# Token tiles of the output projection transposed by DMA in two planes of halves, in place of TensorE

## The chip, the core and the metric

The kernel runs on one core of a Trainium2 chip. The metric is the device time in microseconds, as the median of several runs. The core has a matrix engine (TensorE; PE in the profile, its weight loads PEld), a vector engine (VectorE, DVE), a scalar engine (ScalarE, ACT), GpSimd (POOL) and a queue for transfers (SyncE, SP). Each engine works its own instructions in the order in which they stand, and waits for the others by semaphores. Sixteen DMA engines serve the transfers that SP and ACT issue.

## What is computed

One decoder layer on 256 tokens of width 2048: a SwiGLU half-step, a token mixer of two recurrences (GLA and HGRN2), and a second SwiGLU half-step, each between two RMS norms. The change lies at the end of the mixer:

```python
merged = (sigmoid(z_gla + b[0]) * (o_gla @ w_branch_gla)
          + sigmoid(z_hgrn + b[1]) * (o_hgrn @ w_branch_hgrn))
return merged @ w_out          # (256, 2048) @ (2048, 2048)
```

All matrices and activations are float32.

## The kernel before

**Products.** The 256 tokens are two tiles t = 0, 1 of 128 rows. A product in float32 is made of three matmuls of 128x128 against 128x512 (`mm3`, L158 to L160): every operand is split into a high part in the matrix engine's own format (`hi`, a copy on ACT, L152) and the rest (`lo`, a subtraction on DVE, L154). The weights arrive from DRAM as `raw` (512 KB for 128x1024, issued by SP at L134) and are split into `whi` and `wlo`. Each of the three has a ring of five buffers (`RING`). A weight buffer of 128x1024 is called a chunk here; it feeds twelve matmuls.

**The stage.** `gemm_block` computes the second branch's product `o_hgrn @ w_branch_hgrn` in four blocks n = 0 to 3 of 512 columns: four chunks, 48 matmuls into two banks of PSUM (`mm`, t = 0, 1). After each block, `merge(t, n, b)` runs for both t: at L1257 it multiplies the bank `b` by the gate `s` (tile `sz`) on DVE, at L1258 it adds the other branch's tile `m` (which lies in the home of `h`), both 128x512. So `s` holds merged tokens by columns.

**Transposing.** The output projection `out_proj` needs those tiles with the columns of the model on the partitions, as `xhi` and `xlo` of `mT`. `to_T` makes four transposes on PE against an identity matrix (L398) into a bank of PSUM, and splits that bank: `xhi` on ACT, `xlo` on DVE. A pair of tiles (t = 0, 1) thus costs eight transposes. Then `merge` reloads `h` from its copy in DRAM (L1261, issued by ACT, 256 KB), since `m` lay in its place.

**The projection.** `out_proj` runs 24 chunks (inner tile `kt` 0 to 11 for two halves `hf` of the columns), loaded, split and used in turn, and a tail of eight chunks for `kt` 12 to 15. It accumulates into the eight banks `acc`. `lhs` for tile `kt` pumps the side work until the columns of `kt` are transposed; block n gives `kt` = 4n to 4n + 3.

**What sets the order.** Each engine's queue is set by a scheduler at build time; the kernel's loops give it the program, and the generators in `Side` are stepped between the chunks: `pump` moves each of the light ones by one `yield`, `flush` runs them all to their end. Before the change, `out_proj` calls `side.flush()` once, after its second chunk.

**The pattern that exists already.** In both FFNs `finish` turns the SwiGLU tiles into `hT` by DMA: ACT copies the float32 tile, seen as 16-bit halves, into two planes (`halves`: first all low halves, then all high ones, L708); a transposing DMA of 16-bit elements, issued by ACT, writes `turned` (L712); six steps later ACT copies the planes back, interleaved (`hT`, L717). There are 44 such tiles.

Of the kernel before, what the change touches and what calls it, by code (L numbers as in the profile page):

```python
# [7 lines left out]
F32 = mybir.dt.float32  # L8
# [3 lines left out]
U16 = mybir.dt.uint16  # L12
AF = mybir.ActivationFunctionType
# [3 lines left out]
P = 128  # L17
# [6 lines left out]
CB = 512  # L24
# [63 lines left out]
def kernel(ctx: ExitStack, tc: tile.TileContext, a: dict, out: bass.AP):  # L88
    nc = tc.nc
    side = Side()  # L90
# [7 lines left out]
    work = ctx.enter_context(tc.tile_pool(name="work", bufs=2))  # L98
# [5 lines left out]
    def nm(s):  # L104
        uid[0] += 1
        return f"{s}_{uid[0]}"

    def ps_tile(s="ps"):
        return psum.tile([P, CB], F32, tag="ps", name=nm(s))

    h = [[hpool.tile([P, CB], F32, name=f"h{t}_{n}") for n in range(4)] for t in range(NT)]
# [25 lines left out]
    def wchunk(src: bass.AP, w: int, alloc=ring_alloc, raw=None):  # L137


        raw, apart = raw or wload(src, w)  # L140
        parts = alloc(w)
        if len(parts) == 1:
            hi, lo = parts[0]
            for i in range(2) if apart else [slice(0, 2)]:
                split_into(hi[:, i, :], lo[:, i, :], raw[:, i, :])
            return [(hi[:, i, :], lo[:, i, :]) for i in range(2)]
        for i, (hi, lo) in enumerate(parts):
            split_into(hi, lo, raw[:, i, :])
        return parts

    def split_into(hi, lo, src):
        last[0] = nc.scalar.activation(hi, src, AF.Copy)  # L152
        with tc.issue_after(first_ops.pop().ins) if first_ops else nullcontext():
            nc.vector.tensor_tensor(lo, src, hi.bitcast(F32), op=ALU.subtract)  # L154

    def mm3(ps, x, w, start, stop):
        (xhi, xlo), (whi, wlo) = x, w
        nc.tensor.matmul(ps, lhsT=xhi, rhs=whi, start=start, stop=False)  # L158
        nc.tensor.matmul(ps, lhsT=xlo, rhs=whi, start=False, stop=False)  # L159
        nc.tensor.matmul(ps, lhsT=xhi, rhs=wlo, start=False, stop=stop)  # L160
# [219 lines left out]
    def row_tile(s, dt=F32):  # L380
        return rows.tile([P, 3, CB], dt, tag="row", name=nm(s))

    def load_bcast(t, name, n, after):

        with tc.issue_after(after.ins):
            nc.scalar.dma_start(t, a[name][:, n * CB:(n + 1) * CB].broadcast_to([P, CB]))
# [9 lines left out]
    def transpose4(dst_ps, src, n=4):  # L396
        for i in range(n):
            end = nc.tensor.transpose(dst_ps[:, i * P:(i + 1) * P], src[:, i * P:(i + 1) * P],  # L398
                                      ident)
        return end  # L400

    def tiles4(x):
        return x.rearrange("p (k c) -> p k c", c=P)

    def new_xT():
        x = [None] * NT, [None] * NT, [0] * NT
        for t in range(NT):
            alloc_xT(x, t)
        return x

    def alloc_xT(x, t):
        for part, s in zip(x, ("xhi", "xlo")):
            part[t] = tpool.tile([P, KT, P], F32R, tag=f"{s}{t}", name=nm(f"{s}{t}"))
# [8 lines left out]
    def to_T(x, t, n, src, col=None):  # L422


        ps = ps_tile()
        transpose4(ps, src)
        sl = slice(4 * n, 4 * n + 4)
        v = tiles4(ps)
        if col is not None:
            v = tiles4(work.tile([P, CB], F32, tag="tmp", name=nm("u"), bufs=3))  # L430
            nc.vector.tensor_tensor(v, tiles4(ps), col[:, sl].unsqueeze(2).broadcast_to([P, 4, P]),
                                    op=ALU.mult)
        split_into(x[0][t][:, sl, :], x[1][t][:, sl, :], v)
        x[2][t] = 4 * n + 4
# [100 lines left out]
    def out_proj(w_dram, nkt, lhs, post, scale, pre, homes, following):  # L535

        acc = [[None] * 4 for _ in range(NT)]  # L540
        wpost, free = [], []
        nxt, rs, ready = ([None] * NT, [None] * NT, [0] * NT), [None, None], []

        def load(kt, hf, alloc=ring_alloc):
            return wchunk(w_dram[kt * P:(kt + 1) * P, hf * 1024:(hf + 1) * 1024]
                          .rearrange("p (n c) -> p n c", n=2), CB, alloc)

        def mm(t, n, kt, parts):
            if acc[t][n] is None:
                acc[t][n] = ps_tile(f"acc{t}{n}")  # L550
            mm3(acc[t][n], lhs(t, kt), parts[n % 2], kt == 0, kt == nkt - 1)

        order = [(kt, hf) for hf in range(2) for kt in range(2)]
        order += [(kt, hf) for kt in range(2, nkt - TAIL) for hf in range(2)]
        for i, (kt, hf) in enumerate(order):
            parts = load(kt, hf)
            if 6 <= i < 10:

                if not free:
                    t3 = row_tile("row")  # L560
                    free += [t3[:, j, :] for j in range(3)]
                wpost.append(free.pop(0))
                load_bcast(wpost[-1], post, i - 6, last[0])
            for t in range(NT):
                for n in (2 * hf, 2 * hf + 1):
                    mm(t, n, kt, parts)
            if i == 1:
                side.flush()
        tail = [[(kt, load(kt, hf, homes[hf * TAIL + i]))
                 for i, kt in enumerate(range(nkt - TAIL, nkt))] for hf in range(2)]  # L570

        for t in range(NT):
            ss = small.tile([P, 4], F32, tag="ss", name=nm("ss"))
            for n in range(4):
                for i, (kt, parts) in enumerate(tail[n // 2]):
                    mm(t, n, kt, parts)
                    if i == TAIL // 2 - 1:
                        side.pump()
                square(acc[t][n], ss, n)

                nc.vector.tensor_tensor(acc[t][n], acc[t][n], wpost[n], op=ALU.mult)
                if following is not None and t == 0 and n < AHEAD:
                    ready.append(following(n))
                side.pump()
            side.spawn(settled(t, acc, ss, scale, pre, nxt, rs))
        return nxt, rs, ready
# [89 lines left out]
    def ffn(pre, x, rs, post, pre_next, begin=None, ready=(), then=None):  # L676
        with ExitStack() as fctx:
            fwork = fctx.enter_context(tc.tile_pool(name=nm("fwork"), bufs=2, reuse_waits="tile"))
# [19 lines left out]
            hT = []  # L698
# [3 lines left out]
            def finish(t, f0, w, u, s):  # L702
                n = w // P
                nc.vector.scalar_tensor_tensor(s[:, :w], u[:, :w], rs[t], s[:, :w],
                                               op0=ALU.mult, op1=ALU.mult)
                yield
                halves = fwork.tile([P, 2 * CB], U16, tag="halves", name=nm("halves"))
                nc.scalar.activation(halves[:, :2 * w].rearrange("p (h f) -> p h f", h=2),  # L708
                                     s.bitcast(U16)[:, :2 * w].rearrange("p (f h) -> p h f", h=2),
                                     AF.Copy)  # L710
                turned = work.tile([P, 8, P], U16, tag="tmp", name=nm("turned"), bufs=3)
                nc.scalar.dma_start_transpose(turned[:, :2 * n, :], halves[:, :2 * w])  # L712
                for _ in range(6):
                    yield
                dst = hT[f0 // CB].bitcast(U16)[:, :n, 2 * t * P:2 * (t + 1) * P]
                src = turned[:, :2 * n, :].rearrange("p (h j) k -> p h j k", h=2)
                nc.scalar.activation(dst.rearrange("p j (k h) -> p h j k", h=2), src, AF.Copy)  # L717

            for f0 in range(0, DFF, CB):
                w = min(CB, DFF - f0)  # L720
# [11 lines left out]
                s = []  # L732
# [60 lines left out]
    def mixer(x, rs, ready, following):  # L793
        xl = lhs_of(x)
        w_in = a["w_in"]
        with ExitStack() as mctx:
# [5 lines left out]
            def blk(s, dt=F32):  # L802
                return b2.tile([P, CB], dt, tag="b", name=nm(s), bufs=33)
# [307 lines left out]
            def cols(c0):  # L1111
                return first_of(w_in, c0)
# [64 lines left out]
            k, v, ready = two(O_GK, O_GV, (), cols(O_GV + CB), cols(O_GO))  # L1177
# [8 lines left out]
            go, f, ready = two(O_GO + CB, O_HF, ready, cols(O_HI), cols(O_HO), late=True)  # L1186
# [27 lines left out]
            q, f, ready = two(O_HQ + CB, O_HF + CB, ready, cols(O_HI + CB), cols(O_HO + CB), late=True)  # L1214
# [38 lines left out]
            mT = new_xT()  # L1253

            def merge(t, n, b):
                s, m = szs[n][t], ms[n][t]
                nc.vector.tensor_tensor(s, b, s, op=ALU.mult)  # L1257
                nc.vector.tensor_tensor(s, m, s, op=ALU.add)  # L1258
                yield
                to_T(mT, t, n, s)  # L1260
                nc.scalar.dma_start(m, away[t][n])  # L1261

            side.until(lambda: not side.heavy)
            for n in range(4):
# [105 lines left out]
```

## Time and profile before

| what | us |
|---|---|
| median of 3 runs | 2069.73 (2069.12 to 2075.82) |
| the profiled execution | 2072.41 |
| its span | 2070.3 |
| second branch product, blocks n = 0 to 3, begin at | 1247.15, 1258.15, 1269.93, 1281.73 |
| output projection begins at | 1293.51 |
| the 32 transposes of `sz` lie between | 1260.9 and 1299.7 |

A row of the profile's timeline gives start and length in us from the span's start, engine, line, operation, output and input tile, count, and in brackets the idle time of the engine ahead of it with what ended it. Rows of groups give count, busy us, the mean ns of one, and the idle time with its releasers. PE's lengths overlap, since matmuls are pipelined: the starts tell its pace.

### The profile page before, as it was taken

How to read it: one execution, taken by the hardware profiler on the slowest of the kernel's cores; microseconds unless marked ns; L12 is line 12 of the kernel's file. 1: busy time of each engine (PE TensorE's matmuls, PEld its weight loads, DVE VectorE, ACT ScalarE, POOL GpSimd, SP SyncE). 2: the span in 40 equal slices, each digit the busy share in tenths (PEclk: the TensorE clock that was granted, in tenths of full speed). 3: DMA queues.
4: the chain of work that ended last, by engine and by line, in shares of the span. 5: the costliest groups of instructions: out<-in, count | busy, mean ns of one | idle time of the engine just before them, and what ended most of it. 6: DMA issues, size and time to landing. Idle time of an engine off the chain costs nothing. (4 is left out here: it accounts for less than half of the span.)

```text
span 2070.3 us, 28990 instructions
## 1 busy us (share of the span) xinstructions
PE 2054.9 (99%) x10337; PEld 1701.7 (82%) x10337; DVE 1849.8 (89%) x2187; ACT 1303.3 (63%) x1714; POOL 40.7 (2%) x87
## 2 busy tenths in 40 slices
PE   9999999999999999999999999999999999999998
PEld 7888888888888888878888888888888888888886
DVE  7899998998999879989999897577998999989996
ACT  6666666666666576576655554465666666666663
POOL 1000000000000100000000000010000000000000
PEclk9999999999999999999999999999999999999999
DMA  8776767767667467556565566756767767686663
GB/s 268 204 221 209 242 187 222 217 189 236 212 197 229 153 193 231 163 169 191 171 200 192 180 220 216 220 187 183 219 212 210 214 213 244 176 239 196 217 209 130
DMA packets 246105, 423.50 MB, mean 205 GB/s; under 512 B 63476, under 2 KB 71863, under 8 KB 245960
## 3 DMA queue, kind: packets, MB, share of 16 engines
q1 hardware_dynamic: 194896, 401.80, 61.6%
q10 hardware_dynamic: 51064, 19.84, 4.8%
q8 instruction: 81, 1.33, 0.3%
q14 instruction: 64, 0.52, 0.1%
HBM read 406.11 MB, written 4.19 MB: 198 GB/s over the span
## 5 line engine op out<-in xcount | busy, mean ns | idle before, releaser
L154 DVE TENSOR_TENSOR wlo<-raw,whi 128x1024 fp32r<-128x1024 f32 (+3 forms) x498 | 586.0, 1191 | 83.6 <-ACT whi L152 82.5
L152 ACT ACTIVATE whi<-raw 128x1024 fp32r<-128x1024 f32 (+3 forms) x498 | 507.1, 1031 | 228.9 <-PE c L159 66.2
L158 PE MATMUL c<-whi,xhi 128*128 128x512 f32 (+1 forms) x1270 | 494.0, 389 | 0.0
L160 PE MATMUL c<-wlo,xhi 128*128 128x512 f32 (+1 forms) x1270 | 490.7, 387 | 0.4 <-DVE wlo L154 0.4
L159 PE MATMUL c<-whi,xlo 128*128 128x512 f32 (+1 forms) x1270 | 490.4, 386 | 0.0
L244 DVE TENSOR_TENSOR wlo<-raw,whi 128x1024 fp32r<-128x1024 f32 (+1 forms) x252 | 295.9, 1204 | 35.9 <-ACT whi L283 23.1
L160 PEld LDWEIGHTS c<-wlo,xhi 128*128 128x128 f32 x1270 | 238.4, 188 | 48.0 <-DVE wlo L154 0.9
L158 PEld LDWEIGHTS c<-whi,xhi 128*128 128x128 f32 x1270 | 238.4, 188 | 46.6 <-ACT xhi L470 0.6
L159 PEld LDWEIGHTS c<-whi,xlo 128*128 128x128 f32 x1270 | 238.5, 188 | 45.6
L283 ACT ACTIVATE whi<-raw 128x1024 fp32r<-128x1024 f32 (+1 forms) x126 | 131.6, 1044 | 199.1 <-DVE raw L244 99.6
L244 DVE TENSOR_TENSOR wsuml<-wsum,wsumh 128x1536 fp32r<-128x1536 f32 (+1 forms) x126 | 217.9, 1729 | 8.1 <-ACT wsumh L285 8.1
L160 PE MATMUL c<-wlo,hkhi 128*128 128x512 f32 x558 | 217.2, 389 | 2.4 <-DVE wlo L154 2.0
L159 PE MATMUL c<-whi,hklo 128*128 128x512 f32 x558 | 216.9, 389 | 0.2 <-DVE hklo L154 0.2
L158 PE MATMUL c<-whi,hkhi 128*128 128x512 f32 x558 | 216.8, 389 | 0.0
L281 ACT ACTIVATE wsumh<-wsum 128x1024 fp32r<-128x1024 f32 (+1 forms) x126 | 131.1, 1040 | 88.3 <-DVE wsum L244 65.9
L279 ACT ACTIVATE whi<-raw 128x1024 fp32r<-128x1024 f32 (+1 forms) x126 | 130.9, 1039 | 60.0 <-PE c L159 44.9
L244 DVE TENSOR_TENSOR wsum<-raw,raw 128x1024 f32<-128x1024 f32 (+1 forms) x126 | 151.7, 1204 | 17.8 <-DMA raw<-in_ffn_w_down_dram 13.1
L160 PEld LDWEIGHTS c<-wlo,hkhi 128*128 128x128 f32 x558 | 104.7, 188 | 25.4 <-DVE wlo L154 2.4
L159 PEld LDWEIGHTS c<-whi,hklo 128*128 128x128 f32 x558 | 104.7, 188 | 22.2 <-DVE hklo L154 0.6
L158 PEld LDWEIGHTS c<-whi,hkhi 128*128 128x128 f32 x558 | 104.7, 188 | 21.4
L244 DVE TENSOR_TENSOR c<-c,psum 128x512 f32<-128x512 f32 (+1 forms) x135 | 86.4, 683 | 10.6 <-PE c L160 10.4
L244 DVE TENSOR_TENSOR wsum<-raw 128x512 f32<-128x512 f32 (+1 forms) x126 | 86.1, 683 | 3.6
(346 smaller groups left out, 3156.8 us busy)
## 6 DMA issues: line engine op xcount, KB each, us to landing
raw<-in_ffn_w_down_dram SPq DMA_DIRECT2D x124, 512.0 KB, 5.1
raw<-in_w_in_dram SPq DMA_DIRECT2D x104, 512.0 KB, 4.5
raw<-in_ffn_w_up_dram SPq DMA_DIRECT2D x97, 512.0 KB, 4.4
raw<-in_ffn_w_gate_dram SPq DMA_DIRECT2D x96, 512.0 KB, 4.7
raw<-in_ffn_w_gate_dram SPq DMA_DIRECT2D x128, 256.0 KB, 4.0
raw<-in_w_in_dram SPq DMA_DIRECT2D x128, 256.0 KB, 3.5
raw<-in_ffn_w_up_dram SPq DMA_DIRECT2D x126, 256.0 KB, 3.8
raw<-in_ffn_w_down_dram SPq DMA_DIRECT2D x96, 256.0 KB, 3.6
```

The source lines that it names most:

```text
L152: last[0] = nc.scalar.activation(hi, src, AF.Copy)
L154: nc.vector.tensor_tensor(lo, src, hi.bitcast(F32), op=ALU.subtract)
L158: nc.tensor.matmul(ps, lhsT=xhi, rhs=whi, start=start, stop=False)
L159: nc.tensor.matmul(ps, lhsT=xlo, rhs=whi, start=False, stop=False)
L160: nc.tensor.matmul(ps, lhsT=xhi, rhs=wlo, start=False, stop=stop)
L244: return nc.vector.tensor_tensor(o, x, y, op=op)
L279: nc.scalar.activation(ahi, ra, AF.Copy)
L281: nc.scalar.activation(hi[:, 0:2, :], wsum[:, 0:2, :], AF.Copy)
L283: nc.scalar.activation(bhi, rb, AF.Copy)
```

## The change

Two helpers are taken out of `finish`, and `merge` uses them in place of `to_T`. `turn` is the split into planes and the transposing DMA, `joined` the copy back. In `merge` the copy goes back into `s` itself, three steps later, and `s` is then split into `xhi` and `xlo`. The FFN's instructions stay as they were. In `out_proj` one `pump` after every chunk but the first takes the place of the flush after the second. The tile `halves` comes from the mixer's pool of 33 blocks, `turned` from the pool of three that the FFN uses too.

```diff
+    def turn(src, halves):
+        w = src.shape[-1]
+        halves = halves.bitcast(U16)[:, :2 * w]
+        nc.scalar.activation(halves.rearrange("p (h f) -> p h f", h=2),
+                             src.bitcast(U16).rearrange("p (f h) -> p h f", h=2), AF.Copy)
+        turned = work.tile([P, 8, P], U16, tag="tmp", name=nm("turned"), bufs=3)
+        turned = turned[:, :2 * w // P, :]
+        nc.scalar.dma_start_transpose(turned, halves)
+        return turned
+
+    def joined(dst, turned):
+        nc.scalar.activation(dst.bitcast(U16).rearrange("p j (k h) -> p h j k", h=2),
+                             turned.rearrange("p (h j) k -> p h j k", h=2), AF.Copy)
...
-            if i == 1:
-                side.flush()
+            if i:
+                side.pump()
...
                 nc.vector.tensor_tensor(s, m, s, op=ALU.add)
                 yield
-                to_T(mT, t, n, s)
+                turned = turn(s, blk("halves"))
                 nc.scalar.dma_start(m, away[t][n])
+                yield
+                yield
+                yield
+                joined(tiles4(s), turned)
+                sl = slice(4 * n, 4 * n + 4)
+                split_into(mT[0][t][:, sl, :], mT[1][t][:, sl, :], tiles4(s))
+                mT[2][t] = 4 * n + 4
```

In the changed file the split into planes stands at L409, the transposing DMA at L413, the copy back at L418, the reload of `h` at L1270.

The next rows are ACT's queue before, from the last weight split ahead of the first pair (n = 0) on. `h_0_81` and `h_0_85` are the reloads, `ps` the banks with the transposed tiles.

```order
L152 ACTIVATE whi_11991<-raw_11989 128x1024
L1261 DMA h_0_81<-away_0_89 128x512
L1261 DMA h_0_85<-away_0_93 128x512
L152 ACTIVATE whi_12025<-raw_12023 128x1024
L152 ACTIVATE xhi_2392_11799<-ps_11913 128x512
L152 ACTIVATE xhi_2394_11801<-ps_11921 128x512
L152 ACTIVATE whi_12043<-raw_12041 128x1024
```

And now, at the same place, from the same split on; the `whi` that follow are called A (`whi_12019`) and B.

```order
L152 ACTIVATE whi_11991<-raw_11989 128x1024
L409 ACTIVATE halves_11913<-sz_11039 128x1024
L1270 DMA h_0_81<-away_0_89 128x512
L413 DMA_TRANSPOSE turned_11915<-halves_11913 128x8x128
L409 ACTIVATE halves_11918<-sz_11400 128x1024
L1270 DMA h_0_85<-away_0_93 128x512
L413 DMA_TRANSPOSE turned_11920<-halves_11918 128x8x128
L418 ACTIVATE sz_11039<-turned_11915 128x2x512
L152 ACTIVATE whi_12019<-raw_12017 128x1024
L152 ACTIVATE xhi_2392_11799<-sz_11039 128x512
L418 ACTIVATE sz_11400<-turned_11920 128x2x512
L152 ACTIVATE whi_12037<-raw_12035 128x1024
```

The copy back (L418) waits for a transposing DMA issued just ahead of it, and the weight splits A and B stand behind such copies. Behind B stand the second `xhi`, the splits C and D, and the second pair, built the same way with E and F.

ACT's queue at the third pair (n = 2), now: `turned_12103` and `turned_12108` are its two tiles, G is `whi_12149`, H to J are the three at the end.

```order
L413 DMA_TRANSPOSE turned_12103<-halves_12101 128x8x128
L409 ACTIVATE halves_12106<-sz_11789 128x1024
L1270 DMA h_2_87<-away_2_95 128x512
L413 DMA_TRANSPOSE turned_12108<-halves_12106 128x8x128
L152 ACTIVATE whi_12149<-raw_12147 128x1024
L418 ACTIVATE sz_11410<-turned_12103 128x2x512
L418 ACTIVATE sz_11789<-turned_12108 128x2x512
L152 ACTIVATE xhi_2392_11799<-sz_11410 128x512
L152 ACTIVATE xhi_2394_11801<-sz_11789 128x512
L152 ACTIVATE whi_12177<-raw_12175 128x1024
L152 ACTIVATE whi_12199<-raw_12197 128x1024
L152 ACTIVATE whi_12227<-raw_12225 128x1024
```

One weight split stands between issue and copies; before, this place had the two reloads, one `whi`, the two `xhi` and three `whi`, as at the first pair. At the fourth pair two weight splits (K, L) stand between the issues and the copies, and M is the first behind its `xhi`.

On PE the eight groups of transposes are gone. Those of the fourth pair stood in the output projection, before:

```order
L158 MATMUL acc_2467_12193<-whi_12199,xhi_2394_11801 128x512
L159 MATMUL acc_2467_12193<-whi_12199,xlo_2395_11802 128x512
L160 MATMUL acc_2467_12193<-wlo_12200,xhi_2394_11801 128x512
L398 MATMUL ps_12215<-ident,sz_11412 128x128 x4
L398 MATMUL ps_12223<-ident,sz_11794 128x128 x4
L158 MATMUL acc_2476_12237<-whi_12233,xhi_2392_11799 128x512
```

Now the projection begins so, with the products of `whi` of several accumulators ahead of those of `wlo`:

```order
L158 MATMUL acc_2473_12193<-whi_12177,xhi_2394_11801 128x512
L159 MATMUL acc_2473_12193<-whi_12177,xlo_2395_11802 128x512
L158 MATMUL acc_2484_12231<-whi_12227,xhi_2392_11799 128x512
L159 MATMUL acc_2484_12231<-whi_12227,xlo_2393_11800 128x512
L158 MATMUL acc_2485_12235<-whi_12227,xhi_2392_11799 128x512
L159 MATMUL acc_2485_12235<-whi_12227,xlo_2393_11800 128x512
L160 MATMUL acc_2470_12181<-wlo_12178,xhi_2392_11799 128x512
```

No row between them is a transpose, and four matmuls of the chunk J (`whi_12227`) are drawn ahead of the `wlo` products of H.

More of the change, by code (lines that the diff above doesn't have):

```diff
@@ L706, in finish @@
                 yield
[L707 to L712, printed above, removed]
+                turned = turn(s[:, :w], fwork.tile([P, CB], F32, tag="halves", name=nm("halves")))
                 for _ in range(6):
                     yield
-                dst = hT[f0 // CB].bitcast(U16)[:, :n, 2 * t * P:2 * (t + 1) * P]
-                src = turned[:, :2 * n, :].rearrange("p (h j) k -> p h j k", h=2)
-                nc.scalar.activation(dst.rearrange("p j (k h) -> p h j k", h=2), src, AF.Copy)
+                joined(hT[f0 // CB][:, :n, t * P:(t + 1) * P], turned)
             for f0 in range(0, DFF, CB):
```

## The prediction

> **What bounds the kernel now.** The first two parts of the page come first: is one engine full, and at what clock?
>
> ```profile
> span 2070.3 us, 28990 instructions
> ...
> PE 2054.9 (99%) x10337; PEld 1701.7 (82%) x10337; DVE 1849.8 (89%) x2187; ACT 1303.3 (63%) x1714; POOL 40.7 (2%) x87
> ...
> PEclk9999999999999999999999999999999999999999
> ```
>
> TensorE (PE) is busy in 99% of the span at full clock. So a PE instruction that goes is time won, and every microsecond that PE waits is time lost: no later slack takes it back. The change touches one stage, the four blocks of the second branch product and the start of the output projection. The view by windows gives that stage, with one row for each block and two for pieces of the projection (columns: length, then busy time and count of PE, PEld, DVE, ACT and POOL, clock, DMA share, GB/s).
>
> ```profile
> 1258.15:1269.93 11.78, 11.78 (x58) 9.84 (x56) 8.49 (x11) 5.22 (x6) 0.00 (x0) 1.00 0.72 222
> 1269.93:1281.73 11.80, 11.80 (x57) 9.84 (x56) 8.48 (x11) 5.22 (x6) 0.00 (x0) 1.00 0.75 225
> 1281.73:1293.51 11.78, 11.78 (x58) 9.84 (x56) 8.49 (x11) 5.22 (x6) 0.00 (x0) 1.00 0.73 223
> 1293.51:1316.14 22.63, 22.63 (x104) 18.58 (x103) 13.01 (x14) 9.46 (x10) 0.00 (x0) 1.00 0.79 249
> 1316.14:1337.90 21.76, 21.76 (x97) 18.02 (x96) 9.81 (x8) 8.49 (x8) 0.00 (x0) 1.00 0.63 196
> ```
>
> PE is busy from end to end in every row, and ACT less than half of each. The busy share of ACT hides a limit, though: ACT works its queue in order, and the next rows show how far ahead of PE it is.
>
> ```profile
> 1255.46 1.06 ACT L152 ACTIVATE whi<-raw 128x1024 fp32r<-128x1024 f32 x1 [1.66 <-PE mm L159]
> 1258.18 1.06 ACT L152 ACTIVATE whi<-raw 128x1024 fp32r<-128x1024 f32 x1 [1.66 <-PE mm L159]
> 1259.68 0.94 ACTq L1261 DMA_DIRECT2D h<-away  x2
> 1260.90 1.06 ACT L152 ACTIVATE whi<-raw 128x1024 fp32r<-128x1024 f32 x1 [1.66 <-PE mm L159]
> ```
>
> Each weight split `whi` waits for PE to free a place in the ring of five, so ACT runs at PE's pace, one `whi` every 2.72 us. The one at 1260.90 refills the place of the chunk that PE began at 1258.15. PE needs it five chunks later, at 1258.15 + 5 x 2.72 = **1271.75**: some 9.8 us after it is written. That is the cushion into which new ACT work falls.
>
> **What the change removes.** The transposes of the first pair stand so on PE:
>
> ```profile
> 1260.65 0.39 PE L160 MATMUL mm<-wlo,oT 128*128 128x512 f32 x1
> 1260.88 1.03 PE L398 MATMUL ps<-ident,sz 128*128 128x128 f32 x8
> 1261.67 0.48 PE L158 MATMUL mm<-whi,oT 128*128 128x512 f32 x1
> 1261.98 0.40 PE L159 MATMUL mm<-whi,oT 128*128 128x512 f32 x1
> 1262.22 0.39 PE L160 MATMUL mm<-wlo,oT 128*128 128x512 f32 x1
> ```
>
> Undisturbed matmuls start 0.227 us apart (48 of them: 10.88 us). A block with eight transposes takes 11.78 or 11.80, thus 0.90 more, and the projection's piece with eight 22.63 against 21.76, thus 0.87. Four groups: 0.90 + 0.92 + 0.90 + 0.87 = **3.6 us**, all on the path. The eight copies of `xhi` and eight `xlo` stay, only with another source.
>
> A rule of the Trainium skill (VectorE: DVE Perf Modes, "Rules for kernel authors") speaks against this change: it sends a 128x128 transpose to TensorE where PSUM may be the destination, and otherwise to the DMA. The same page's section "The three transpose paths" puts the former at 390 ns; 32 of them would be an estimated 12.5 us, and the sum below would come out 1.3 us faster than before. The windows say 0.11 us for each, and the measurement decides.
>
> **What it adds.** Per pair of tiles (t = 0, 1) ACT gets two splits into planes (`halves`), two transposing DMAs, and two copies back (`sz<-turned`, here J0 and J1). Both FFNs do the same to `hT`, so these rows have their durations, from the views by tile of `halves` and `turned`:
>
> ```profile
> L708 ACT ACTIVATE halves<-silu x44: 828/1042/1060, 55.3 to 1837.1; 128x1024 uint16<-128x1024 uint16 x40, 128x768 uint16<-128x768 uint16 x4
> L712 ACTq DMA_TRANSPOSE turned<-halves x44: 1227/1292/2006, 56.3 to 1838.5; - x44
> L717 ACT ACTIVATE hT<-turned x44: 1062/1361/1394, 61.7 to 1847.5; 128x1024 uint16<-128x1024 uint16 x40, 128x768 uint16<-128x768 uint16 x4
> DMA to landing us min/median/max: 2.8/5.1/8.9
> ```
>
> So 1.04 us for a split, 1.29 for an issue (which must wait for its split, and holds what stands behind it), 1.36 for a copy, and between issue and landing L = 2.8 to 8.9, median 5.1. Even without a wait this fills ACT: 2 x (1.04 + 1.29 + 1.36) for the pair, 4 x 0.96 for the `whi` and 2 x 0.53 for the `xhi` are 12.3 us a block against PE's 10.88. And on top ACT **waits** for each landing, with the next `whi` queued behind. In the FFN such a wait looks like this:
>
> ```profile
> 1562.57 1.39 ACT L717 ACTIVATE hT<-turned 128x1024 uint16<-128x1024 uint16 x1 [0.45 <-DMA turned<-halves]
> 1566.10 1.37 ACT L717 ACTIVATE hT<-turned 128x1024 uint16<-128x1024 uint16 x1 [2.14 <-DMA turned<-halves]
> 1567.33 1.03 ACT L152 ACTIVATE whi<-raw 128x1024 fp32r<-128x1024 f32 x1
> ```
>
> There three or four splits stand between issue and copy. Here, by the new order of ACT's queue, none does in the first two pairs, one in the third, two in the fourth.
>
> I follow that queue. An instruction behind another on ACT starts about 0.1 us before the first one's end (`whi` at 1250.02 for 1.06, the next at 1250.98), so the steps are 0.96 for `whi`, 1.26 for J, 0.53 for `xhi` (two in 1.06).
>
> ```profile
> 1250.02 1.06 ACT L152 ACTIVATE whi<-raw 128x1024 fp32r<-128x1024 f32 x1
> 1250.98 0.62 ACT L1027 ACTIVATE sz<-sz 128x512 f32<-128x512 f32 x1
> ...
> 1261.86 1.06 ACT L152 ACTIVATE xhi<-ps 128x512 fp32r<-128x512 f32 x2
> ```
>
> From a pair's start: split 1.04, issue to 2.33, second split to 3.37, second issue to 4.66.
> - Pair 0: J0 at 1.04 + L, `whi` A, `xhi`, J1 at 3.79 + L, `whi` B, `xhi`, `whi` C and D; the next pair begins at 8.46 + L.
> - Pair 1: the same with two `whi` (E, F): 6.54 + L.
> - Pair 2: `whi` G during the wait, J0, J1 at 3.37 + L (its own DMA left 2.33 later), two `xhi`, `whi` H, I, J: 8.57 + L.
> - Pair 3: `whi` K and L, J0, J1 at 3.37 + L, two `xhi`, and `whi` M is done at 6.75 + L.
>
> Pair 0 starts at 1259.68, where ACT now sends the reload of `h`, which waits for the same sum. M is done at 1259.68 + 30.3 + 4L. PE wants M twelve chunks after A, at 1271.75 + 12 x 2.72 = 1304.4. Behind M stands its `wlo` on DVE (1.22 us), which PE wants 0.45 after M: 0.77 more. Together **PE is late by 4L - 13.6 us**. With L = 5.1 that is 6.8: 1.7 for F, 1.2 for G, 3 for H, the rest for M. Each microsecond of landing counts four times, since four waits stand in a row on one queue. The next rows are the stage's groups on DVE, and from the list of DMA issues the reload of `h`.
>
> ```profile
> L154 DVE TENSOR_TENSOR wlo<-raw,whi 128x1024 fp32r<-128x1024 f32 x25 | 30.5, 1224 | 22.7 <-ACT whi L152 22.7
> L154 DVE TENSOR_TENSOR xlo<-ps,xhi 128x512 fp32r<-128x512 f32 x8 | 5.1, 683 | 0.0
> ...
> h<-away ACTq DMA_DIRECT2D x8, 256.0 KB, 3.5
> ```
>
> DVE's own queue adds nothing: the sum that pair 1 needs stands behind `xlo` of pair 0 and is done at about 7.9 + L, before 8.46 + L; the same margin holds later.
>
> **Which L.** The trace has no transpose of `sz`. From below, 2.8 us; from above, 8.9. I take 5.1 and add 1.1, because each transpose has a reload of `h` just ahead in ACT's DMA queue: 256 KB at the stage's 223 GB/s, an estimate. L = 6.2 makes PE late by 11.2, less 3.6 removed: **7.6 us slower**. Should the cushion not be there, each pair would cost PE the wait in full; it is in the formula as the 13.6.
>
> **Edits at nothing.** Stepwise pumping in place of the flush only moves the last pair's splits: its columns (inner tile 12 on) are read after 24 chunks of the projection, 65 us on. FFN lines only call the new helpers; same instructions. The eight transposes (2 MB) add about a tenth of what the stage's DMA moves, and its share is 0.72 to 0.79.
>
> **Rivals.**
> 1. *The transposes land fast and the cushion holds* (not slower). With L up to 3.4 the formula gives no lateness, only the removal is left: 3.6 us faster, 2066. For it: a plain DMA of the same 256 KB from the same queue lands in 3.5, and the fastest transposes in 2.8. Against it: the median of 5.1 under weight traffic of the same strength. The Trainium skill (Advanced Engine Details and Errata, "X-Bar Transpose (TRN2)") says that transposing DMAs are as fast as regular ones; that rule is this rival, and this trace, 5.1 against 3.5, speaks against it. The sides change at L = 4.3, where the lateness equals the 3.6 us removed.
> 2. *The transposes land late.* After a wait ACT frees several raw buffers at once, SP sends that many 512 KB weight loads, and they share the engines with the next transpose. At L = 8 PE is late by 18.4, and the kernel 14.8 us slower: 2084.5. For it: landings up to 8.9, where a pair is sent into running loads. Against it: here a pair's DMAs leave 2.3 us apart, not 1.3.
>
> That the change doesn't do what it says is no rival: all eight groups of transposes are gone from PE's queue.
>
> **How the numbers follow.** The profiled execution took 2072.41, its span 2070.3; the median of three runs is 2069.73, 2.7 lower. The forecast gives 2072.41 + 7.6 = 2080.0 for such an execution, and 2069.73 + 7.6 = 2077.3 on the median's scale, which I use. About 0.3%, 6.2 us, is what a measurement of this kernel can tell from no change; the forecast passes that at L = 5.84. Chances: forecast (L 4.3 to 7.4, nothing to 12.4 slower) 0.65, rival 1 0.18, rival 2 0.17. Slower by over 0.3%: all of rival 2 and 0.38 of the forecast, 0.55. Within 0.3%: 0.43. Faster by over 0.3% would need more than all that is removed: 0.02. The range 2066.5 to 2086 reaches from rival 1 to L = 8.4 and leaves out the ends of both.
>
> **What would show it.** Right: in the windows from 1269 to 1312 blocks longer than 10.88, the lateness beginning with the third block; ACT idle before `sz` on the copy's line, ended by the DMA `turned`; PE waiting for `whi` or `wlo` of L152 and L154; landings near 6. Wrong: all blocks at 10.88 and a span 3.6 shorter (rival 1), landings of 8 and weight loads in bursts (rival 2), or waits at another place, a PSUM bank or DVE. The forecast stands or falls with the eight landings.

## The result, and the profile after

| | median, us | runs |
|---|---|---|
| after | 2083.57 (2078.61 to 2086.99) | 6 |
| before, beside it | 2071.95 (2069.12 to 2076.2) | 6 |

The ratio is 1.0053, with a 95% interval of 1.0041 to 1.0066: the change costs 8.5 to 13.7 us. The forecast was 7.6 slower. The profiled execution of after took 2081.05 us. Its page begins with the span and then the busy time of the engines:

```profile
span 2078.9 us, 28953 instructions
...
PE 2055.8 (99%) x10305; PEld 1702.7 (82%) x10305; DVE 1849.4 (89%) x2187; ACT 1320.2 (64%) x1730; POOL 40.7 (2%) x87
```

The 32 transposes are gone (10337 matmuls before, 10305 now), and little else on the page tells that the kernel lost: PE still shows 99%, since some 10 us of waiting are half a per cent of the span. The view by windows tells it. Its rows for after are the four blocks, the wait ahead of the projection, and the projection up to its 192nd matmul in two pieces (columns as in the prediction).

```profile
1246.72:1257.73 11.01, 11.01 (x51) 9.10 (x50) 9.16 (x12) 6.97 (x10) 0.00 (x0) 1.00 0.60 185
1257.73:1268.61 10.88, 10.88 (x49) 9.01 (x48) 3.23 (x5) 3.18 (x3) 0.00 (x0) 1.00 0.94 152
1268.61:1283.96 15.35, 13.36 (x49) 9.91 (x48) 9.02 (x11) 9.53 (x11) 0.00 (x0) 0.89 0.65 156
1283.96:1301.07 17.11, 13.03 (x48) 9.67 (x47) 7.16 (x9) 9.96 (x11) 0.00 (x0) 0.90 0.87 206
1301.07:1304.15 3.08, 0.39 (x3) 0.01 (x1) 1.70 (x4) 3.08 (x5) 0.00 (x0) 1.00 0.37 118
1304.15:1328.76 24.61, 23.85 (x96) 18.95 (x96) 15.65 (x16) 15.28 (x16) 0.00 (x0) 0.93 0.86 270
1328.76:1350.52 21.76, 21.76 (x98) 18.02 (x96) 11.03 (x9) 9.55 (x9) 0.00 (x0) 1.00 0.75 247
```

The second block now takes 10.88, without transposes, and is still in step. The third takes 15.35, the fourth 17.11, and 3.08 more pass before the projection starts. From the first block's start to the end of the last row it is 103.80 us; before, from 1247.15 to 1337.90, it was 90.75. So the stage lost **13.05 us**, and PE, from which 3.6 us of transposes were taken, is 16.65 late. (The rest of the span, with the same 3229 matmuls, came out shorter in this execution: 728.38 against 732.40 before. In the traces of the other kernels of this study, which have the same instructions there, it is 729.3 to 733.1. So most of this difference is the spread between executions; that none of it comes from the change is not shown.)

The next rows are ACT's timeline in after, at the first pair:

```profile
1260.34 1.28 ACTq L413 DMA_TRANSPOSE turned<-halves  x1
...
1270.27 1.36 ACT L418 ACTIVATE sz<-turned 128x1024 uint16<-128x1024 uint16 x1 [7.54 <-DMA turned<-halves]
1271.50 1.03 ACT L152 ACTIVATE whi<-raw 128x1024 fp32r<-128x1024 f32 x1
```

The first transpose is issued at 1260.34, and ACT stands still for 7.54 us until it has landed. Only then comes the weight split, which PE wants by 1271.33 in this execution (its second block began at 1257.73; five chunks of 2.72 later). The list of waits says who waited in the stage from the first pair on, first for ACT (1259.2 to 1320.1), then for PE (1246.7 to 1328.8):

```profile
ACT sz L418 <- DMA turned<-halves: 17.4, 5, 7.5
ACT halves L409 <- DVE wlo L154: 4.1, 3, 1.4
ACT whi L152 <- issue: 2.8, 2, 1.5
ACT halves L409 <- DVE sz L1267: 1.8, 2, 1.3
```

```profile
PE acc L158 <- ACT whi L152: 3.2, 2, 2.7
PE mm L160 <- DVE wlo L154: 3.2, 3, 2.3
PE mm L158 <- ACT whi L152: 2.9, 2, 1.8
PE acc L160 <- DVE wlo L154: 0.3, 1, 0.3
```

ACT waits 17.4 us for landings and not once for PE; the three other rows are mostly the time in which it issues a DMA (mostly 1.25 to 1.43 us each, not counted as busy). Before, it waited mostly for PE, 16.6 us of it in this row of the same view (1259.2 to 1305):

```profile
ACT whi L152 <- PE mm L159: 16.6, 10, 1.7
```

So the roles are exchanged: in this stage ACT's queue sets the pace and PE follows. How long a transfer took stands in the list of DMA issues for 1258 to 1318 (count of issues, and the median from the start of the issue to the landing):

```profile
turned<-halves ACTq DMA_TRANSPOSE x8, 7.4
```

Eight transposes were issued, but the records have the landing of only five: 9.9, 8.4, 5.2, 5.6 and 7.4 us. A sixth can be read from the copy that waited for it: the transpose issued at 1278.58 was awaited until 1283.76, thus 5.2. The median of these six is 6.5, not 7.4. (Of the other two, the one issued at 1293.15 was shorter still: its copy began at 1297.80 without a wait.) So every landing given below comes with the number of landings that it rests on.

### The profile page after: what moved, and what is told of

Same layout as the page of the kernel before. It is cut to its first block, busy times and chain, and to the rows that moved or that the text cites. A ratio compares the mean times of both kernels' runs of the same rounds, so it can differ in the third digit from the quotient of the medians.

```text
span 2078.9 us, 28953 instructions
## 1 busy us (share of the span) xinstructions
PE 2055.8 (99%) x10305; PEld 1702.7 (82%) x10305; DVE 1849.4 (89%) x2187; ACT 1320.2 (64%) x1730; POOL 40.7 (2%) x87
## 5 line engine op out<-in xcount | busy, mean ns | idle before, releaser
L154 DVE TENSOR_TENSOR wlo<-raw,whi 128x1024 fp32r<-128x1024 f32 (+3 forms) x498 | 585.3, 1190 | 83.4 <-ACT whi L152 79.8
L152 ACT ACTIVATE whi<-raw 128x1024 fp32r<-128x1024 f32 (+3 forms) x498 | 506.2, 1030 | 205.2 <-PE c L159 71.7
L244 DVE TENSOR_TENSOR wsum<-raw,raw 128x1024 f32<-128x1024 f32 (+1 forms) x126 | 151.6, 1203 | 17.9 <-DMA raw<-in_ffn_w_down_dram 13.7
```

The lines of the kernel that those rows point to most:

```text
L244: return nc.vector.tensor_tensor(o, x, y, op=op)
```

## The experiments

Every kernel was timed beside the kernel before. The stage is measured in the profiled execution as above, from the first block's first matmul to the start of the projection's 192nd; before, it is 90.75 in the first trace and 90.74 in that of the run with the pump alone.

| kernel | ratio to before, 95% | us against before | stage, us | landings read: count, median, longest, us |
|---|---|---|---|---|
| after | 1.0053 (1.0041 to 1.0066) | +11.0 | 103.80 | 6, 6.5, 9.9 |
| more steps | 1.0005 (0.9988 to 1.0022) | +1.0 | 89.62 | 3, 9.6, 10.0 |
| no transfer | 0.9983 (0.9974 to 0.9992) | -3.5 | 86.94 | none |
| late reload | 1.0125 (1.0109 to 1.0141) | +25.9 | 115.45 | 8, 5.7, 12.5 |
| pump alone | 1.0000 (0.9990 to 1.0009) | 0.0 | 90.74 | none |
| more steps, late reload | 0.9985 (0.9976 to 0.9994) | -3.1 | 89.01 | 7, 9.1, 10.7 |
| copy on GpSimd | 1.0008 (0.9993 to 1.0023) | +1.7 | 102.3 | 5, 9.4, 18.8 |
| pairs 1 and 3 alone | 1.0052 (1.0033 to 1.0070) | +10.8 | 101.27 | 3, 10.7, 11.8 |
| small reload | 1.0051 (1.0034 to 1.0068) | +10.6 | 102.34 | 5, 7.0, 11.5 |
| plain copies | 1.0018 (1.0009 to 1.0028) | +3.7 | 94.69 | 7, 4.5, 7.5 |
| one weight | 0.9989 (0.9980 to 0.9998) | -2.3 | 88.48 | 4, 3.1, 3.2 |

The third column is the ratio less one, times the median of before (2071.4 to 2072). The last takes in the landings in the list of DMA issues and, where that has none, the time from an issue to the copy that waited for its landing; it is one execution of each kernel. The medians that the list itself gives rest on fewer landings, and differ. The four kernels in the rows behind after alter one thing each.

**More steps between transfer and copy.**

```diff
                 turned = turn(s, blk("halves"))
                 nc.scalar.dma_start(m, away[t][n])
-                yield
-                yield
-                yield
+                for _ in range(8):
+                    yield
                 joined(tiles4(s), turned)
```

> The kernel after, but with eight steps instead of three between the transposing DMA and the copy back, so that in each pair three or more weight splits stand on ACT between the issues and the copies. If PE is late because weight splits stand behind copies that wait for a landing (theory), ACT's 17.4 us of idle time on the copy's line should fall below 6, the half-clock windows of this stage should go, and the time should lie 3 us below to 3 us above the kernel before (after: 11 above). If ACT's added work is too much by itself, whatever the order (rival: 12.3 us a block against PE's 10.88, 5.6 us over four blocks), the stage stays late by 5 us or more. If the landings get longer as they are given more room (rival: the weights that ACT frees earlier load into them), the idle time on the copies stays above 10 us and the time 6 us or more above before.

The time came out level with before. The rows are PE's waits in the stage:

```profile
PE acc L160 <- DVE wlo L154: 1.0, 2, 0.5
PE acc L158 <- ACT whi L152: 0.4, 1, 0.4
PE mm L160 <- DVE wlo L154: 0.2, 1, 0.2
```

The three landings on record took 10.0, 9.6 and 5.4 us, so they were no shorter than in after, and PE waited 1.6 us instead of 9.6; ACT's idle time on the copies fell from 17.4 to 2.4. So it isn't the landing by itself that costs, but what stands behind the wait for it. ACT's work is all there, in the same amount, so that rival falls too.

**No transfer.**

```diff
-                turned = turn(s, blk("halves"))
+                turned = turn(s, blk("halves"), dma=False)
...
+        if not dma:
+            return halves.rearrange("p (j k) -> p j k", k=P)
```

> The kernel after without the eight transposing DMAs of the merged tiles: the copy back reads the two planes where ACT wrote them. Left out: the transposing itself (the projection multiplies untransposed tiles) and eight issues of 1.29 us on ACT. ACT's splits and copies, the reloads and all matmuls stay. If the wait for landings is the cause (theory), PE is no longer late and only the removal of 32 transposes is left: 3.6 us below before, at most level with it. If ACT's work alone makes PE late (rival), 2 x (1.04 + 1.36) more a block, without the issues 9.7 us against PE's 10.88, the time stays 5 us or more above before. If the order of the projection's first matmuls or the stepwise pumping is the cause (rival), it stays at 8 to 11 above.

3.5 us faster (1.7 to 5.4): the size of the removal, 3.6. (The issues are gone here too; more steps, which keeps them, shows that they are not the cause.) The window of the last block shows both engines:

```profile
1277.76:1288.64 10.88, 10.88 (x50) 9.01 (x48) 8.98 (x11) 9.38 (x11) 0.00 (x0) 1.00 0.73 226
```

Without transfers ACT is busy 9.38 us in a block of 10.88, and PE works without a wait.

**The reload behind the split, and the pump alone.**

```diff
-                nc.scalar.dma_start(m, away[t][n])
                 yield
                 yield
                 yield
                 joined(tiles4(s), turned)
...
                 mT[2][t] = 4 * n + 4
+                nc.scalar.dma_start(m, away[t][n])
```

> The kernel after with the reload of h (256 KB) issued behind the split of the turned tile instead of ahead of the next transpose. The two copies of a pair then stand directly behind each other on ACT, without a weight split between them. If the reload ahead in ACT's DMA queue lengthens the landing (a step of the prediction: 1.1 us each; in the trace of after the first landing took 9.9 us beside reloads of 9.1 and 7.8), the median landing of these eight falls by 1 to 4 us and the time to 2 to 7 us above before. If the weights of SP's queue alone set the landing (rival), landings stay between 5 and 10 and the time at 9 to 13 above before.

26 us slower, outside both expectations. The new order explains a part: the second copy now stands directly behind the first, and no weight split between. The other part is seen at the second pair (ACT's timeline, then SP's):

```profile
1273.47 2.84 ACTq L413 DMA_TRANSPOSE turned<-halves  x2
1276.34 1.12 ACTq L1277 DMA_DIRECT2D h<-away  x2
1278.86 1.37 ACT L418 ACTIVATE sz<-turned 128x1024 uint16<-128x1024 uint16 x1 [4.47 <-DMA turned<-halves]
1286.04 1.34 ACT L418 ACTIVATE sz<-turned 128x1024 uint16<-128x1024 uint16 x1 [5.81 <-DMA turned<-halves]
```

```profile
1274.02 1.50 SPq L134 DMA_DIRECT2D raw<-in_w_branch_hgrn_dram  x2
1276.29 0.34 SPq L134 DMA_DIRECT2D raw<-in_w_out_dram  x1
```

Three weight loads of 512 KB leave within 2.6 us, because three splits had come one after another; the second transpose, issued at 1274.81 between them, is used only at 1286.04. That is the burst of the prediction's second rival. It is not alone, though. The program issues the reloads behind the split, but in ACT's queue they stand right behind the two transposes and ahead of the copies (1276.34), so they share the DMA with the second transpose. At the first pair two reloads follow as well, but no burst stood there, and the two transposes landed in 5.5 and 4.9. Three of the eight landings took over 11 us.

For the pump, the line `if i == 1: side.flush()` of before became `if i: side.pump()`, and nothing else was changed.

> The kernel before with only the stepwise pumping in place of the flush in the projection; transposes stay on PE. The prediction set this at nothing: within 2 us of before. If the stepwise pumping itself disturbs the start of the projection (rival), 3 us or more above before, with PE waits behind the first chunks of the projection.

Ratio 1.0000: it costs nothing.

**More steps and the late reload together** (both diffs above).

> Eight steps between transfer and copy back as in the run with more steps, and the reload of h issued behind the split as in the run with the late reload. That run alone (late reload) was 26 us slower, with both copies of a pair directly behind the issues and up to 5.8 us of idle time before a copy; here at least one weight split stands between issues and copies in every pair. If what is queued behind the waiting copy decides (theory), PE's waits in the stage stay below 1 us and the time is 1 to 4 us below before. If the late reload itself is what hurts (rival: it now shares the DMA with the next pair's transposes), the time is 5 us or more above before, with landings over 8.

Faster than before by 3.1 us (1.2 to 5.0), and so faster than both kernels. PE's waits in the stage are 1.3 us, a little more than expected:

```profile
PE acc L158 <- ACT whi L152: 0.8, 1, 0.8
PE acc L160 <- DVE wlo L154: 0.5, 1, 0.5
```

Four of the seven landings that can be read took over 9 us: the sign that the rival named came, without its time. The same late reload costs 26 us in one order of ACT's queue and nothing in the other.

**The copy back on GpSimd.**

```diff
+        if on_pool:
+            nc.gpsimd.tensor_copy(dst.bitcast(U16).rearrange("p j (k h) -> p h j k", h=2),
+                                  turned.rearrange("p (h j) k -> p h j k", h=2))
+            return
...
-                joined(tiles4(s), turned)
+                joined(tiles4(s), turned, on_pool=True)
+                for _ in range(5):
+                    yield
```

> The kernel after with the copy back on GpSimd (busy 2% so far) instead of ACT, and the split five steps later; splits into planes, issues and reloads stay on ACT. No weight split stands behind a wait for a landing any more. If the cause is ACT's queue behind the landing (theory), ACT's idle time ended by a transposing DMA is gone in this stage, PE waits less than 2 us, and the time is 3.6 below to 1 above before. No trace so far shows how long GpSimd takes for such a copy: up to about 5 us (two copies in a block of 10.88 us) it is hidden; if it takes longer (rival), xhi of the last pairs waits for it and ACT's queue stands behind that, 3 us or more above before. If the landings themselves, through shared DMA, hold the weights up (second rival), the time stays 5 or more above whatever engine copies.

At the median it is no longer slow, but not faster than before either, which lies between the forecasts of the theory and the first rival; single runs went from 2069.14 to 2085.05. The profile caught that slowest one, so its stage in the table is no typical one. A copy on GpSimd takes 1.38 us at the median, so its length is no hindrance. What is left is the wait, handed on to `xhi`, behind which weight splits stand again (ACT's timeline):

```profile
1302.66 0.63 ACT L152 ACTIVATE xhi<-sz 128x512 fp32r<-128x512 f32 x1 [4.48 <-POOL sz L418]
1312.36 0.63 ACT L152 ACTIVATE xhi<-sz 128x512 fp32r<-128x512 f32 x1 [9.06 <-POOL sz L418]
```

**Pairs 1 and 3 alone by DMA.**

```diff
+                if n % 2 == 0:
+                    to_T(mT, t, n, s)
+                    nc.scalar.dma_start(m, away[t][n])
+                    return
                 turned = turn(s, blk("halves"))
```

> The kernel after with only the pairs n = 1 and 3 transposed by DMA; n = 0 and 2 go over TensorE as before. ACT's queue at n = 1 and n = 3 stands as it does in after at n = 0, with the second copy and four weight splits behind the first wait. If lateness comes from waits in a row that use up one cushion of 9.8 us (theory), ACT makes up the cushion in the block between (11.78 us with 5.2 busy) and the two pairs cost PE nothing to 3 us: with 16 transposes less (1.8 us) the time is 2 below to 1 above before. If every pair costs its own share (rival), half of the 11 us that after loses stays: 4 to 7 above before.

A miss for both: half the transposes cost 10.8 us, about as much as all of them. The rows are ACT's timeline at pair 1 and PE's largest wait:

```profile
1283.56 1.34 ACT L418 ACTIVATE sz<-turned 128x1024 uint16<-128x1024 uint16 x1 [9.42 <-DMA turned<-halves]
```

```profile
PE ps L398 <- DVE sz L1267: 7.5, 1, 7.5
```

This one wait, 9.42 us with a full cushion ahead of it, uses it up; four in a row aren't needed. And the kernel has a dependence that after doesn't have: the transposes of pair 2, still on PE, wait for a sum on DVE, DVE for the weight split on ACT, and ACT for the landing.

**A small reload.**

```diff
-                nc.scalar.dma_start(m, away[t][n])
+                nc.scalar.dma_start(m[:, :16], away[t][n][:, :16])
```

> The kernel after with the reload of h cut from 512 to 16 columns (8 KB for 256 KB) at its place; left out are the other 496 columns of the residual. ACT's queue at the first pair is row for row that of after, so this run tests the reload ahead in ACT's DMA queue by itself. If it lengthens the landing (the prediction's 1.1 us; 9.9 for the first transpose of after, with reloads of 9.1 and 7.8 beside it), the first landing falls to 5 or 6, and the time to 1 to 6 us above before. If the weight loads alone set the landing (rival), the first landing stays at 8 to 10 and the time at 9 or more above.

ACT's timeline at the first pair, and at the second copy of the second pair:

```profile
1262.27 1.27 ACTq L413 DMA_TRANSPOSE turned<-halves  x1
...
1267.64 1.37 ACT L418 ACTIVATE sz<-turned 128x1024 uint16<-128x1024 uint16 x1 [3.00 <-DMA turned<-halves]
```

```profile
1279.58 1.25 ACTq L413 DMA_TRANSPOSE turned<-halves  x1
...
1291.08 1.34 ACT L418 ACTIVATE sz<-turned 128x1024 uint16<-128x1024 uint16 x1 [5.12 <-DMA turned<-halves]
```

From issue to copy it is now 5.37 us at the first pair, where after has 9.93 (1260.34 to 1270.27), and ACT's wait there fell from 7.54 to 3.00: the reload did lengthen this landing, by some 4.5 us. The time did not follow. At the second pair, where ACT's order differs a little (one weight split stands between the two issues), a transpose issued at 1279.58 is used 11.5 us later. The waits put down to landings come to 17.4 us in all, as in after. The theory of the reload explains one landing, not the loss.

**Plain copies, and one weight.** Together with after these two separate the kind of transfer from the traffic beside it.

```diff
-        nc.scalar.dma_start_transpose(turned, halves)
+        if plain:
+            nc.scalar.dma_start(turned, halves.rearrange("p (j k) -> p j k", k=P))
+        else:
+            nc.scalar.dma_start_transpose(turned, halves)
...
-                turned = turn(s, blk("halves"))
+                turned = turn(s, blk("halves"), plain=True)
```

> The kernel after with eight plain DMAs from the planes to turned in place of the eight transposing ones: same bytes, same queue, same waits, reloads and weight loads as they are. Left out: the transposing itself. If it is the transposing that makes a transfer late beside other traffic (theory: in after, transposes, reloads and a weight load together, 1.5 MB, take 10 us, and in the run with pairs 1 and 3 alone 11.8), the landings fall to 3 to 5 us, PE waits less than 2 us in the stage, and the time is 3.6 below to 2 above before. If it is only the amount that is in flight (rival: 256 KB share the DMA engines with up to three loads of 512 KB), the landings stay at 5 to 10 and the time at 6 to 13 above before.

```diff
+            one[0] = wload(a["w_branch_hgrn"][2 * P:4 * P, :CB]
+                           .rearrange("(k p) c -> p k c", p=P), CB)
             for n in range(4):
                 b = gemm_block(a["w_branch_hgrn"], n * CB, CB, o_lhs("h"), nkt=8, ready=ready,
+                               raws=one * 4)
...
-            parts = load(kt, hf)
+            parts = load(kt, hf, raw=one[0] if i < 12 else None)
```

> The kernel after with one weight buffer loaded ahead of the four blocks and split again and again for the chunks of these blocks and for the first twelve of the projection. Left out: the loads of 15 + 12 weight chunks (their values are those of one chunk). Splits, matmuls, transposing DMAs and reloads stay, in ACT's order up to one weight split. If transposing DMAs are late because of the weight traffic beside them (theory), they land in 3 to 5.5 us and PE waits less than 3 us: 3.6 below to 2 above before. If they are late by themselves or through the reloads in their own queue (rival), the first landing stays at 9 to 12, as in after, and the time at 5 or more above before.

The first fence has PE's waits with the plain copies, the second rows of the list of DMA issues with the single weight (medians of four landings each):

```profile
PE mm L160 <- DVE wlo L154: 2.8, 1, 2.8
PE acc L158 <- ACT whi L152: 1.2, 1, 1.2
```

```profile
h<-away ACTq DMA_DIRECT2D x8, 256.0 KB, 2.7
...
turned<-halves ACTq DMA_TRANSPOSE x8, 3.1
```

Without weight loads a transposing DMA lands in 3.1 us beside reloads that need 2.7, and the kernel is 2.3 us faster than before, as the theory said. The plain copies meet neither forecast in full: they land in 2.6 to 7.5 us, 4.5 at the median of seven, PE waits 4.0 us, and the time is 3.7 above before. A transposing one beside weight loads, in after, needs 5.2 to 9.9, 6.5 at the median of six. So beside the weight traffic a transposing DMA lands some 3.4 us later than without it, and some 2 us later than a plain copy beside the same traffic, in one execution each. Of these 2 us, 0.8 is the longer issue (1.29 us against 0.47 on ACT, and a landing is counted from the start of the issue). That issue also takes ACT's time, so the 7 us between this kernel and after aren't all due to landings.

What transposing does to the DMA engines can be read from the lists of their queues. The rows are the queue of ACT's transfers, first in after (1258 to 1318), then with the plain copies (1258 to 1310): packets, MB, and the share of the time of all sixteen engines.

```profile
q10 hardware_dynamic: 9600, 4.20, 37.8%
```

```profile
q10 hardware_dynamic: 2304, 4.20, 25.8%
```

Both are eight reloads and eight turned tiles, the same 4.20 MB. In after they take 37.8% of 60 us, thus 22.7 us of all sixteen engines; with plain copies 25.8% of 52 us, thus 13.4. By this estimate each transposing DMA takes about 1.2 us more of the engines, which the weight loads share. Its packets are smaller: of all packets in the window, 8787 of 12069 are under 512 B in after, 467 of 4818 with plain copies. That this is why transposing DMAs land later under load is argued; no run tested it. The rule of the Trainium skill ("Advanced Engine Details and Errata", section "X-Bar Transpose (TRN2)") that transposing DMAs are as fast as regular ones nearly holds here for the landing without weight loads, 3.1 against 2.7 for a reload. It does not hold for the time that they take of the engines.

## Why the prediction came out as it did

- **PE is the bound and each transpose removed is time won**: right. Without transfers, 3.5 us of the 3.6 are there.
- **ACT's order, not its busy share, decides**: right, and shown by three runs. With the same work and landings no shorter, more steps take away the loss; without transfers it is gone; and without weight traffic it is gone.
- **Where it begins**: right. Block two is in step, block three takes 4.47 us more than 10.88, PE waits for `whi` and `wlo` on L152 and L154, ACT on L418. Within the third block PE waits sooner than by the queue that the prediction followed, at A and not at F, since the first landing was 9.9 and not 6.2.
- **The formula, late by 4L - 13.6**: its steps along ACT's queue are right, and it left out one wait. It counts the first landing of pairs 0 and 1 and the second of pairs 2 and 3. Here these were 9.9, 5.2, 5.2 and 7.4, together 27.7, where four times 6.2 is 24.8; 27.7 - 13.6 is 14.1. The rows are the copies that waited in after, behind the one at 1270.27:

```profile
1283.76 1.37 ACT L418 ACTIVATE sz<-turned 128x1024 uint16<-128x1024 uint16 x1 [2.76 <-DMA turned<-halves]
...
1289.41 1.35 ACT L418 ACTIVATE sz<-turned 128x1024 uint16<-128x1024 uint16 x1 [2.86 <-DMA turned<-halves]
...
1300.80 1.35 ACT L418 ACTIVATE sz<-turned 128x1024 uint16<-128x1024 uint16 x1 [1.63 <-DMA turned<-halves]
...
1316.76 1.37 ACT L418 ACTIVATE sz<-turned 128x1024 uint16<-128x1024 uint16 x1 [2.66 <-DMA turned<-halves]
```

  The copy at 1289.41 is the second of pair 1. The prediction let it run directly behind `xhi`; here it waited 2.86 us more for its own transpose, which was issued at 1281.04 and landed after 8.4. So there were five waits in a row and not four: 14.1 + 2.9 is 17.0, and PE was 16.65 late. It is a rule for this order alone: one landing of more than the cushion was enough when only two pairs were transposed.
- **The size, 7.6**: too small. The time is 11.0 above before (8.5 to 13.7); in the stage of the profiled execution PE is 16.65 late where 11.2 was forecast. The missing 5.4 are the two terms above, 2.9 for the landings that count and 2.9 for the fifth wait, less 0.3 that the sum does not explain.
- **L = 6.2**: near in size, not in its making, and so in part luck. The four landings that count have a mean of 6.9, but single ones go from 5.2 to 9.9, and the 1.1 for the reload ahead is no steady term: at the first pair its share was 4.5 (9.93 against 5.37), one execution each. The estimate took the reload's bytes at the stage's 223 GB/s; while reloads, transposes and a weight load ran together, 1260.3 to 1270.3 in after, the list of DMA issues shows this mean:

```profile
DMA packets 2123, 1.51 MB, mean 151 GB/s; under 512 B 1571, under 2 KB 1571, under 8 KB 2123
```

  And where no reload stood ahead, bursts of weight loads came with other late transposes (late reload, small reload), as the second rival said. Two of the six landings read in after are over that rival's 8.
- **The reload as the cause of landings**: too simple. Making it small, or moving it, doesn't win the time back. What the two have in common is the weight traffic, and only without it do landings fall to 3.1.
- **The eight transposes as a tenth of what the DMA moves**: true of the bytes only. They take more of the engines' time than plain transfers of their size, 22.7 against 13.4 us for the same 4.20 MB.
- **The 0.11 us for a transpose on PE, against 390 ns**: the section of the Trainium skill that the prediction cites ("VectorE: DVE Perf Modes", "The three transpose paths") gives its figure for bf16, and these are float32, in a stream with other matmuls. The 3.5 us won without transfers bear out the 0.11.
- **The pump for the flush costs nothing**: right, 1.0000.
- **Rival 1** (landings up to 3.4, no lateness, 3.6 faster) did not come about in after, but the run with one weight is that case: landings of 3.1, PE's wait 1.0 us, 2.3 faster.

Open is why transposing DMAs land later than plain copies beside weight loads, and which transfer of several in flight comes out last. Beside weight loads the single transposes that can be read landed between 4.9 and 12.5 us from their issue, and one after 18.8, in the slowest execution of the copy on GpSimd.

## What to carry to other kernels

A wait costs what stands behind it on the same engine: before an operation is moved to an asynchronous transfer, look at the queue of the engine that picks the result up, and put enough independent work between issue and use to cover the longest landing seen under load, not the median. Here five more steps and a later reload turned 11 us lost into 3 us won, with the same instructions. Where an in-order engine feeds the bound one, its busy share says little: ACT was at 64% of the span while it set the pace.

## What the runs showed of the hardware that was not expected

In this stage PE's granted clock fell to half three times for 3.41 us, each time after a stretch of the same length with much waiting. Two rows of the view by windows of after, for the first of them (the others follow stretches with 0.73 us of PE work, at 1291.06 and 1301.30):

```profile
1270.58:1273.99 3.41, 1.80 (x8) 0.86 (x7) 1.43 (x2) 3.41 (x4) 0.00 (x0) 1.00 0.17 38
1273.99:1277.41 3.42, 3.42 (x9) 2.65 (x10) 3.27 (x6) 3.42 (x5) 0.00 (x0) 0.50 0.46 153
```

In this stage each stretch with 1.80 us or less of PE work out of 3.41 is followed by one at 0.50. Its matmuls start 0.43 us apart (1275.59, 1276.02) instead of 0.227. The window from 1318.37, with 2.65 busy, was followed by full speed. PE's busy time alone doesn't decide it, though: with pairs 1 and 3 alone by DMA, a window with less, elsewhere in the kernel, was followed by full speed.

```profile
459.81:463.22 3.41, 1.47 (x7) 0.89 (x5) 2.29 (x3) 3.24 (x5) 0.00 (x0) 1.00 0.09 37
463.22:466.63 3.41, 3.27 (x14) 2.74 (x15) 3.41 (x7) 1.67 (x2) 0.00 (x0) 1.00 0.92 162
```

The Trainium skill ("TensorE: Matmul & The Clock Gate", section "Part 1: The HAM clock gate") describes a free-running window of 3413 ns and a half clock after an idle window; the length agrees, but here the half clock also followed a window that was about half idle. Where the limit lies is open.

Three such stretches with about 27 matmuls at 0.2 us more each are about 5 us. By the list of waits they were not added to the loss in after: ACT did not wait for PE between 1259.2 and 1320.1 (DVE did, twice, 3.2 us in all, but what ACT needed next stood behind splits that waited longer), and PE waited for ACT's split once more at 1320.12, behind the last slow stretch. At full clock PE would have waited there instead. That is argued from the waits; no run tested it.
